# Two places for the front's weight blocks instead of four, the first weights ahead of other transfers, HGRN levels one block later, and only the last row of the last w_down by columns

## The chip, the cores and the metric

One core of a Trainium2 chip runs the whole program. The metric is the device time of one execution in microseconds. Weights come from HBM over 16 DMA engines that the core's queues share; TensorE (PE) multiplies, ScalarE (ACT) and VectorE (DVE) prepare operands and take results, GpSimd (POOL) does small work, and SyncE (SP) issues nearly all transfers, one after the other in the order of the program.

## What the kernel computes

One block of a transformer in float32, 256 tokens of width 1024. The front is a projection of the normed input and two mixers (sparse attention "NSA" and the gated recurrence "HGRN2") whose outputs are merged; then a mixture of 32 experts follows, of which every token uses two:

```
h = rmsnorm(x, attn_norm)
proj = h @ w_in                      # q, kv, gates | hg q, f, i, g | merge
o_nsa = nsa_mixer(...)               # compressed, selected and window attention
o_hg = rmsnorm(hgrn2_mixer(q, f, i, lb), hg_norm) * silu(g)
mixed = sigmoid(m0) * (o_nsa @ w_br_nsa) + sigmoid(m1) * (o_hg @ w_br_hg)
x = x + mixed @ w_out
t = rmsnorm(x, ffn_norm)
x = x + sum_e combine[:, e] * ((silu(t @ w_gate[e]) * (t @ w_up[e])) @ w_down[e])
return rmsnorm(x, final_norm)
```

The experts' weights are 32 x 3 matrices of 2 MB. All of them are read once, whichever tokens choose them.

## The kernel before, in words

**The front.** The weights of the front come in 30 blocks of up to 128x2048 values, in this order: f0, f1, q0, q1 (HGRN forget and query), c0, c1, b0, b1, a0, a1 (NSA), i0, i1, g0, g1 (HGRN value and gate), m20 to m31, h0, h1, m00 to m11, n0, n1 (merge gates and branch outputs), o00, o10, o01, o11 (w_out). Each block takes the same way. SyncE loads it (1.05 MB, tile `raw`, L268, in `load_front`). ScalarE copies it to a value of fewer bits, "hi" (L282), and VectorE takes the rest, "lo" (L286), both into a tile `wsp` (`split`). TensorE then makes a float32 product of three products: hi by hi (L442), hi by lo (L444), lo by hi (L445), in groups of four (`three`), four groups for a block (half as long in c0 and c1). A split runs a block or more ahead of the products, and as its last step it issues the load of a later block into the place that it has read. The raw places are a ring of four halves of two 2 MB buffers.

**Fillers.** Behind each group `run` takes steps from a list (`fill`): the steps of HGRN and NSA. HGRN's are two `hg_diag` (product at L574, then a predicated copy on VectorE) and seven levels of `hg_mm` (product at L600) and `hg_update` (L616, L617, L620 on VectorE); each level's product needs the update of the level before.

**Places for weights.** One pool of eleven 2 MB buffers ("w2", `pair`) holds everything of that size: the raw ring, the `wsp` tiles, the transposed input `hhl`, and the experts' weights. A request takes the buffer that comes free first by the planned order, and a load into it waits for the last reader of what was there. A second pool of three 1 MB buffers ("w", `slot`) holds `x`, the masks `lmf`, `wcm`, the residual's x and w_down's halves `wh`.

**Weights ahead.** `EARLY` says how many pieces of the experts' weights are issued when a block of the front starts. The first quad of experts (24 MB in all) comes as pieces k0 to k3 (a quarter of w_gate's rows for all four experts, L321), u0 to u3 (w_up, L326), and d0, d1, d2 and two halves of the fourth w_down (L331, L339). What isn't loaded early is issued by the experts' products as they free buffers. A SyncE instruction that waits for its buffer holds up all that stand behind it.

**Experts.** Eight quads: gate products `pg` (L1258), up products `pu`, then `py` (L1315), each by four experts side by side. In the last quad w_down is loaded in the parts of `LAST` (L352): rows are the four slices of w_down's rows, columns the output's. `down_last` multiplies rows 0 and 1 for all columns, then rows 2 and 3 in three spans of columns (512, 256 and 256); each span is scaled (`weighted`, L1298 and L1299), added to the output by a product (`scatter`, L1304), squared and normed.

**Start.** SyncE's first transfers are xb (half of the transposed input), f0 in two halves, f1, the vectors and constants, x, q0, the masks and q1. A semaphore lane of a transfer is used again eight transfers later, so eight are under way at most.

## Time and profile before

| | |
|---|---|
| runs shown, lowest, median, highest | 680.13, 681.19, 682.99 us |
| the profiled execution | 680.27 us, span 678.3 us |
| mean granted TensorE clock in it | 0.898 of full speed |
| PE, DVE, ACT busy | 81%, 31%, 21% of the span |
| DMA | 238.84 MB, mean 352 GB/s |
| first expert product to end of span | 243.79 to 678.3 us |

The span is what the engines' records cover; some 2.0 us of the execution lie outside it. The page cuts the span into 40 slices of 17 us: PE is at 8 or 9 tenths through the first 14, the front, while DMA stands at 119 to 254 GB/s in most of slices 3 to 11; from slice 14 on DMA is at 9 tenths or more and PE between 4 and 8. In a timeline each line is one instruction or a run of like ones: its start, its length, engine, line, operation, what it writes and reads, and in brackets how long its engine was idle before it and what released it.

### The profile page before, as it was taken

The page shows a single profiled execution, that of the slowest core. Times are in us where ns is not written, and L with a number is a line of the kernel's source. Part 1 is how long each engine was busy: PE and PEld are TensorE (multiplying, and loading weights), DVE is VectorE, ACT ScalarE, POOL GpSimd, SP SyncE. Part 2 cuts the span into 40 slices and gives each one's busy share as a digit, 9 for nine tenths or more (in the row PEclk, how much of TensorE's full clock was granted, in tenths as well). Part 3 has the DMA queues.
Part 4 walks back from the last instruction along what each step waited for, and adds up shares of the span by engine and source line. Part 5 has one row for each costly group of instructions (what it writes and reads, how often), then busy time and mean ns, then how long its engine had stood idle before and what let it go on. Part 6 is the DMA issues. An engine that isn't in the chain of part 4 may idle for free.

```text
span 678.3 us, 8658 instructions
## 1 busy us (share of the span) xinstructions
PE 548.6 (81%) x3692; PEld 314.8 (46%) x3692; DVE 212.8 (31%) x430; ACT 145.4 (21%) x235; POOL 32.0 (5%) x50
## 2 busy tenths in 40 slices
PE   8989999999999999987758468766846877594574
PEld 6988777888898854342114114212411421141121
DVE  5686856777558342121002102101210110020012
ACT  5433348466455310100000000000000000000003
POOL 0411500200000000000000000000000000000001
PEclk8999999999999999989679788967968796697888
DMA  8856463463578999999999999999999999999993
GB/s 343 346 190 229 143 254 119 151 230 129 191 269 320 425 421 427 427 422 431 427 428 427 426 426 426 429 425 432 423 426 431 422 429 428 426 427 429 420 389 119
DMA packets 26443, 238.84 MB, mean 352 GB/s; under 512 B 2720, under 2 KB 5280, under 8 KB 10144
## 3 DMA queue, kind: packets, MB, share of 16 engines
q1 hardware_dynamic: 26112, 237.44, 84.9%
q8 instruction: 31, 0.51, 0.3%
q10 hardware_dynamic: 288, 0.79, 0.3%
q14 instruction: 12, 0.10, 0.0%
HBM read 237.17 MB, written 1.05 MB: 351 GB/s over the span
## 4 chain that ended last, share of the span: by engine, by line
DMA 50%; PE 29%; DVE 1%; ACT 0%; issue 0%; SPq 0%; POOL 0%; POOLq 0%; DVEq 0%; ACTq 0%
DMA we<-in_w_up 20%; DMA we<-in_w_gate 15%; DMA wh<-in_w_down 10%; DMA wd<-in_w_down 6%; PE pu L1258 5%; PE pws L442 3%; PE pws L445 3%; PE pws L444 3%; PE pg L1258 2%; PE py L1315 2%; PE pga L1146 2%; PE pwo L442 1%; PE pwo L445 1%; PE pwo L444 1%; PE pno L903 1%; PE pnt L880 1%
## 5 line engine op out<-in xcount | busy, mean ns | idle before, releaser
L1258 PE MATMUL pg<-we,xe 128*32 128x512 f32 x512 | 94.3, 723 | 52.1 <-DMA we<-in_w_gate 52.1
L1258 PE MATMUL pu<-we,xe 128*32 128x512 f32 x512 | 91.2, 721 | 47.3 <-DMA we<-in_w_up 43.5
L1286 DVE SCALAR_TENSOR_TENSOR h<-pu,wv,h 128x512 f32<-128x512 f32 x8 | 8.7, 1089 | 246.2 <-PE pu L1258 246.2
L286 DVE TENSOR_TENSOR wsp<-raw,wsp 128x2048 fp32r<-128x2048 f32 (+3 forms) x34 | 68.2, 2011 | 33.7 <-ACT wsp L282 33.5
L1258 PEld LDWEIGHTS pg<-we,xe 128*32 128x32 f32 x512 | 20.1, 128 | 121.7 <-DMA we<-in_w_gate 73.4
L1258 PEld LDWEIGHTS pu<-we,xe 128*32 128x32 f32 x512 | 20.4, 129 | 113.1 <-DMA we<-in_w_up 61.9
L282 ACT ACTIVATE wsp<-raw 128x2048 fp32r<-128x2048 f32 (+3 forms) x34 | 56.3, 1663 | 45.0 <-PE pws L445 14.9
L1298 ACT ACTIVATE ys<-py,wv 128x512 fp32r<-128x512 f32 (+1 forms) x17 | 11.3, 663 | 243.2 <-PE py L1315 211.8
L1315 PE MATMUL py<-wh,hT 128*32 128x512 f32 x112 | 49.4, 594 | 3.7 <-DMA wh<-in_w_down 3.7
L1315 PE MATMUL py<-wd,hT 128*32 128x512 f32 x336 | 50.6, 595 | 0.0
L445 PE MATMUL pws<-hhl,wsp 128*128 128x256 f32 x192 | 49.3, 288 | 0.7 <-DVE wsp L286 0.7
L444 PE MATMUL pws<-hhl,wsp 128*128 128x256 f32 x192 | 49.1, 287 | 0.0
L1280 ACT ACTIVATE h<-pg,wv 128x512 f32<-128x512 f32 x8 | 9.2, 1144 | 150.6 <-PE pg L1258 150.6
L445 PEld LDWEIGHTS pws<-hhl,wsp 128*128 128x128 f32 x192 | 37.4, 195 | 1.0 <-DVE wsp L286 0.9
L444 PEld LDWEIGHTS pws<-hhl,wsp 128*128 128x128 f32 x192 | 37.4, 195 | 0.0
L442 PE MATMUL pws<-hhl,wsp 128*128 128x256 f32 x192 | 34.1, 297 | 1.3 <-ACT hhl L401 1.3
L1299 DVE SCALAR_TENSOR_TENSOR ys<-py,wv,ys 128x512 fp32r<-128x512 f32 (+1 forms) x17 | 12.2, 719 | 69.0 <-ACT ys L1298 68.4
L1146 PE MATMUL pga<-lm,x 128*128 128x128 f32 x256 | 30.3, 276 | 0.0
L444 PE MATMUL pxs<-wsp,hhl 128*128 128x512 f32 (+1 forms) x80 | 29.9, 377 | 0.2 <-DVE wsp L286 0.2
L442 PEld LDWEIGHTS pws<-hhl,wsp 128*128 128x128 f32 x192 | 27.3, 194 | 5.1 <-ACT hhl L401 2.4
L445 PE MATMUL pxs<-wsp,hhl 128*128 128x512 f32 (+1 forms) x80 | 29.5, 372 | 0.0
L1146 PEld LDWEIGHTS pga<-lm,x 128*128 128x128 f32 x256 | 29.3, 192 | 0.2 <-DVE lm L1137 0.2
(252 smaller groups left out, 684.3 us busy)
## 6 DMA issues: line engine op xcount, KB each, us to landing
we<-in_w_gate SPq DMA_DIRECT2D x32, 2048.0 KB, 34.3
we<-in_w_up SPq DMA_DIRECT2D x32, 2048.0 KB, 34.5
wd<-in_w_down SPq DMA_DIRECT2D x21, 2048.0 KB, 39.1
raw<-in_wf SPq DMA_DIRECT2D x27, 1024.0 KB, 4.8
wh<-in_w_down SPq DMA_DIRECT2D x15, 1024.0 KB, 30.0
wd<-in_w_down SPq DMA_DIRECT2D x3, 1024.0 KB, 35.6
wd<-in_w_down SPq DMA_DIRECT2D x3, 512.0 KB, 23.6
wd<-in_w_down SPq DMA_DIRECT2D x6, 256.0 KB, 8.6
```

Of the source, the lines that this page charges most:

```text
L282: i = S.activation(his[n][:, c], raws[n][:, c], AF.Copy)
L286: splits.append((i, V.tensor_tensor(los[n][:, c], raws[n][:, c], his[n][:, c].bitcast(F32), op=OP.subtract)))
L442: PE.matmul(out_, lh, rh, start=start and i == 0, stop=False, skip_group_check=True)
L444: PE.matmul(out_, lh, rl, start=False, stop=False, skip_group_check=True)
L445: last = PE.matmul(out_, ll, rh, start=False, stop=stop and i == n - 1, skip_group_check=True)
L1146: i = PE.matmul(pgs[q, n][:, 128 * k:128 * k + 128], xv[:, tt, 512 * n + 128 * k:512 * n + 128 * k + 128], sel[q][:, tt], start=tt == 0 an ...
L1258: i = PE.matmul(p[32 * e:32 * e + 32], xes[q][:, k, 32 * e:32 * e + 32], W["k", k // 2][:, e, k % 2] if by_rows else W[4 * q + e][:, k], s ...
L1280: S.activation(h, pg.rearrange("p (c j) -> p c j", j=4), AF.Silu, scale=r)
L1286: V.scalar_tensor_tensor(h, pu.rearrange("p (c j) -> p c j", j=4), r, h, op0=OP.mult, op1=OP.mult)
L1298: return (S.activation(hi[:, c], p[:, c], AF.Copy, scale=wv), V.scalar_tensor_tensor(lo[:, c], p[:, c], wv, hi[:, c].bitcast(F32), op0=OP. ...
L1299: V.scalar_tensor_tensor(lo[:, c], p[:, c], wv, hi[:, c].bitcast(F32), op0=OP.mult, op1=OP.subtract))
L1315: PE.matmul(py[n][32 * e:32 * e + 32], hTs[q][:, j, 32 * e:32 * e + 32], WD[4 * q + e, j][:, 512 * n:512 * n + 512], start=j == 0, stop=j ...
```

## The change

The raw ring has two places, halves of one 2 MB buffer, so ten buffers are left for the rest where there were nine. `EARLY` adds two pieces in b0 and n0 and n1 and takes one from i1, 11 in all instead of 9; one more filler per group runs in m20. f0's first half is issued ahead of xb, and vectors, constants, x, masks and wcm are issued behind the latest block. The copy of the token factors (rxb) is put behind VectorE's latest split. In c the first four groups take no filler. `LAST` loads row 2 whole and row 3 in three parts of columns, and `down_last` multiplies rows 0, 1 and 2 for all columns first, and row 3 span by span. The last quad's w_down takes 20 transfers where it took 16: four of 1.05 MB, four of 524 KB, four of 262 KB and eight of 131 KB (before: four of 1.05 MB, four of 524 KB, eight of 262 KB).

```diff
--- before.py
+++ after.py
@@ -171,11 +171,12 @@
 YSB = 4
 WHOLE = slice(0, 512)
 CUTS = [slice(0, 256), slice(256, 512)]
-LAST = [(slice(0, 2), slice(0, 1024)), (slice(2, 4), slice(0, 512)), (slice(2, 4), slice(512, 768)), (slice(2, 4), slice(768, 1024))]
+LAST = [(slice(0, 2), slice(0, 1024)), (slice(2, 3), slice(0, 1024)), (slice(3, 4), slice(0, 512)),
+        (slice(3, 4), slice(512, 768)), (slice(3, 4), slice(768, 1024))]
 GATE_V = (0, 0)
-EARLY = {"a0": 1, "i1": 1, "m31": 1, "m10": 1, "n0": 1, "o00": 1, "o10": 1, "o01": 2}
+EARLY = {"b0": 1, "a0": 1, "m31": 1, "m10": 1, "n0": 2, "n1": 1, "o00": 1, "o10": 1, "o01": 2}
 HOLD = 3
-FILLS = {"n0": 2, "m10": 3, "m20": 1, "m11": 3, "m01": 3, "m00": 3, "h0": 1, "h1": 1, "i": 1, "m30": 1, "g": 1}
+FILLS = {"n0": 2, "m10": 3, "m20": 2, "m11": 3, "m01": 3, "m00": 3, "h0": 1, "h1": 1, "i": 1, "m30": 1, "g": 1}
 
 
 @with_exitstack
@@ -255,24 +256,27 @@
 
     ident = C("ident")
     raws, his, los, marks, splits = {}, {}, {}, [], []
-    ring = [h for _ in range(2) for h in two(pair("raw"), 2048)]
+    ring = two(pair("raw"), 2048)
+    last_dma = []
     to_load, to_split = list(FRONT), list(FRONT)
+
+    def after(i):
+
+        return tc.issue_after(getattr(i, "ins", i))
 
     def load_front():
         if to_load:
             n = to_load.pop(0)
             w = WIDTH[n]
-            raws[n] = ring[FRONT.index(n) % 4][:, :w]
+            raws[n] = ring[FRONT.index(n) % 2][:, :w]
             step = w // 2 if n == FRONT[0] else w
             for o in range(0, w, step):
-                nc.sync.dma_start(raws[n][:, o:o + step], bass.AP(tensor=wf.tensor, offset=wf.offset + FOFF[n] + 128 * o,
-                                                                  ap=[[step, 128], [1, step]]))
+                i = nc.sync.dma_start(raws[n][:, o:o + step], bass.AP(tensor=wf.tensor, offset=wf.offset + FOFF[n] + 128 * o,
+                                                                      ap=[[step, 128], [1, step]]))
+                last_dma.append(i)
                 if n == FRONT[0] and o == 0:
-                    nc.sync.dma_start(xs[1][:, :1024], xb)
-
-    def after(i):
-
-        return tc.issue_after(getattr(i, "ins", i))
+                    with after(i):
+                        nc.sync.dma_start(xs[1][:, :1024], xb)
 
     def split_part(n, c, behind=()):
 
@@ -353,15 +357,16 @@
 
     load_front()
     load_front()
-    nc.sync.dma_start(vc_, vec)
-    nc.sync.dma_start(cs, consts[:, :kept])
-    xv = load_x("x", x)
-    load_front()
-    nc.sync.dma_start(cm_[:, :consts.shape[1] - kept], consts[:, kept:])
-    hgn = row("hgn", cm_[:, 384:])
-    brow = row("br", cp.tile([128, 36], F32, name="brow"))
+    with after(last_dma[-1]):
+        nc.sync.dma_start(vc_, vec)
+        nc.sync.dma_start(cs, consts[:, :kept])
+        xv = load_x("x", x)
     lmf = slot("lmf")[:, :1152].rearrange("p (l t) -> p l t", l=9)
-    nc.sync.dma_start(lmf, lmask)
+    with after(last_dma[-1]):
+        nc.sync.dma_start(cm_[:, :consts.shape[1] - kept], consts[:, kept:])
+        hgn = row("hgn", cm_[:, 384:])
+        brow = row("br", cp.tile([128, 36], F32, name="brow"))
+        nc.sync.dma_start(lmf, lmask)
 
 
     hh_, hl_ = two(pair("hhl", F32R), 2048)
@@ -423,7 +428,8 @@
         prx = bank("ns", "prx")
         with after(marks[-3]):
             PE.matmul(prx[:, :256], one.to_broadcast([128, 128]), rxd, start=True, stop=True)
-        V.tensor_copy(rxb, prx[:, :256])
+        with after(splits[-1][1]):
+            V.tensor_copy(rxb, prx[:, :256])
 
     rt = VC("rt").rearrange("p (k e) -> p k e", k=8)
     G.memset(ones, 1.0)
@@ -432,7 +438,8 @@
         G.tensor_copy(before, lmf[:, 8])
         G.tensor_tensor(rt, rt, VC("fe")[:, :, None].to_broadcast([128, 8, 36]), op=OP.mult)
     wcm = slot("wcm")
-    nc.sync.dma_start(wcm, wcmp)
+    with after(last_dma[-1]):
+        nc.sync.dma_start(wcm, wcmp)
     dump("hT", hhi.bitcast(F32))
 
 
@@ -950,7 +957,10 @@
     hg += [(hg_cross,)]
     for a in hg:
         later(*a)
-    run(project("c", evac_c, 280))
+    gen = project("c", evac_c, 280)
+    for _ in range(4):
+        next(gen)
+    run(gen)
     ns = [(ns_cT, 0), (ns_cT, 1), (ns_blk, 0), (ns_blk, 1)]
     todo[4:4] = [(a[0], a[1:]) for a in ns]
     run(project("b", evac_b))
@@ -1335,9 +1345,9 @@
                               skip_group_check=True)
 
         for i in range(3):
-            products(i, (0, 1))
+            products(i, (0, 1, 2))
         for i, (n, c) in enumerate(spans):
-            products(i, (2, 3))
+            products(i, (3,))
             if i < 2:
                 ys = parts_of()
             weighted(q, n, c, py[i], ys)
```

SyncE, the first transfers of the program, before (`raw` is a block of the front: f0 in two halves, f1, then q0, then q1):

```order
L271 DMA xab<-in_xb 128x1024
L268 DMA raw<-in_wf 128x1024 x2
L268 DMA raw<-in_wf 128x2048
L356 DMA vc__69<-in_vec 128x328
L357 DMA cs<-in_consts 128x202
L229 DMA x<-in_x 128x1024 x2
L268 DMA raw<-in_wf 128x2048
L360 DMA cm__71<-in_consts 128x384
L245 DMA cm__71<-in_rows 128x128
L245 DMA brow<-in_rows 128x36
L364 DMA lmf<-in_lmask 128x1152
L268 DMA raw<-in_wf 128x2048
```

and with the change:

```order
L274 DMA raw<-in_wf 128x1024
L279 DMA xab<-in_xb 128x1024
L274 DMA raw<-in_wf 128x1024
L274 DMA raw<-in_wf 128x2048
L361 DMA vc__69<-in_vec 128x328
L362 DMA cs<-in_consts 128x202
L230 DMA x<-in_x 128x1024 x2
L366 DMA cm__71<-in_consts 128x384
L246 DMA cm__71<-in_rows 128x128
L246 DMA brow<-in_rows 128x36
L369 DMA lmf<-in_lmask 128x1152
L274 DMA raw<-in_wf 128x2048 x2
```

xb goes behind f0's first half, and q0 from ahead of the constants and masks (its place was row 7) to behind them, beside q1.

TensorE at the start of block c, before (`pxs` is c's product, `phl` a step of HGRN):

```order
L442 MATMUL pxs<-wsp,hhl 128x280 x2
L444 MATMUL pxs<-wsp,hhl 128x280
L445 MATMUL pxs<-wsp,hhl 128x280
L444 MATMUL pxs<-wsp,hhl 128x280
L445 MATMUL pxs<-wsp,hhl 128x280
L574 MATMUL phl<-hg_360,hg 128x128 x4
L442 MATMUL pxs<-wsp,hhl 128x280 x2
L444 MATMUL pxs<-wsp,hhl 128x280
L445 MATMUL pxs<-wsp,hhl 128x280
L444 MATMUL pxs<-wsp,hhl 128x280
L445 MATMUL pxs<-wsp,hhl 128x280
L574 MATMUL phl<-hg_360,hg 128x128 x4
```

and with the change, where four groups of c stand ahead of these rows:

```order
L449 MATMUL pxs<-wsp,hhl 128x280 x2
L451 MATMUL pxs<-wsp,hhl 128x280
L452 MATMUL pxs<-wsp,hhl 128x280
L451 MATMUL pxs<-wsp,hhl 128x280
L452 MATMUL pxs<-wsp,hhl 128x280
L581 MATMUL phl<-hg_358,hg 128x128 x4
L449 MATMUL pxs<-wsp,hhl 128x280 x2
L451 MATMUL pxs<-wsp,hhl 128x280
L452 MATMUL pxs<-wsp,hhl 128x280
L451 MATMUL pxs<-wsp,hhl 128x280
L452 MATMUL pxs<-wsp,hhl 128x280
L581 MATMUL phl<-hg_358,hg 128x128 x4
```

The first two steps of HGRN are drawn after the fifth and the sixth group of c instead of after the first and the second.

SyncE, end of the front, before (from the last two blocks but one: `we` are pieces of w_gate and w_up, `wd` and `wh` of w_down):

```order
L268 DMA raw<-in_wf 128x2048 x2
L326 DMA we<-in_w_up 128x4096
L268 DMA raw<-in_wf 128x2048
L326 DMA we<-in_w_up 128x4096
L229 DMA x_1985<-in_xp 128x1024 x2
L326 DMA we<-in_w_up 128x4096 x2
L331 DMA wd<-in_w_down 128x4096
L339 DMA wh<-in_w_down 128x2048
L331 DMA wd<-in_w_down 128x4096 x2
L339 DMA wh<-in_w_down 128x2048
```

and with the change:

```order
L274 DMA raw<-in_wf 128x2048 x2
L330 DMA we<-in_w_up 128x4096
L274 DMA raw<-in_wf 128x2048
L330 DMA we<-in_w_up 128x4096
L274 DMA raw<-in_wf 128x2048
L330 DMA we<-in_w_up 128x4096
L230 DMA x_1987<-in_xp 128x1024 x2
L274 DMA raw<-in_wf 128x2048
L330 DMA we<-in_w_up 128x4096
L335 DMA wd<-in_w_down 128x4096
L343 DMA wh<-in_w_down 128x2048
L335 DMA wd<-in_w_down 128x4096 x2
```

Two of the last three blocks now stand behind the second and third piece of w_up, and o11 behind x.

## Rows read from the trace of the kernel before

**Rows 1.** the page's costliest groups; columns as its line 5 says

```profile
L1258 PE MATMUL pg<-we,xe 128*32 128x512 f32 x512 | 94.3, 723 | 52.1 <-DMA we<-in_w_gate 52.1
L1258 PE MATMUL pu<-we,xe 128*32 128x512 f32 x512 | 91.2, 721 | 47.3 <-DMA we<-in_w_up 43.5
```

**Rows 2.** stretches: from:to, sum, PE, PEld, DVE, ACT, POOL busy, PEclk, DMA share, GB/s

```profile
10.00:20.00 10.00, 10.00 (x73) 9.89 (x72) 8.69 (x17) 7.43 (x12) 0.90 (x2) 0.83 0.91 354
208.00:209.00 1.00, 1.00 (x11) 1.00 (x10) 1.00 (x2) 0.67 (x1) 0.00 (x0) 1.00 0.02 8
210.00:246.00 36.00, 35.54 (x241) 29.43 (x243) 20.54 (x58) 11.02 (x23) 2.01 (x6) 1.00 0.99 412
250.00:260.00 10.00, 10.00 (x80) 3.07 (x72) 2.12 (x7) 2.47 (x2) 0.00 (x0) 1.00 1.01 426
655.00:660.00 5.00, 3.78 (x48) 1.84 (x52) 1.07 (x2) 0.00 (x0) 0.00 (x0) 1.00 1.04 365
660.00:665.00 5.00, 4.85 (x40) 1.49 (x32) 0.75 (x1) 0.69 (x1) 0.00 (x0) 1.00 0.81 264
```

**Rows 3.** timeline of SyncE's queue, end of the front: start, length, instruction

```profile
199.50 0.33 SPq L268 DMA_DIRECT2D raw<-in_wf  x1
209.62 0.33 SPq L326 DMA_DIRECT2D we<-in_w_up  x1
...
245.77 5.48 SPq L326 DMA_DIRECT2D we<-in_w_gate  x4
```

**Rows 4.** timeline of ScalarE, start: start, length, instruction, idle before and releaser

```profile
7.10 0.63 ACT L282 ACTIVATE wsp<-raw 128x512 fp32r<-128x512 f32 x1 [4.44 <-DMA raw<-in_wf]
...
16.76 1.92 ACT L282 ACTIVATE wsp<-raw 128x2048 fp32r<-128x2048 f32 x1 [1.34 <-DMA raw<-in_wf]
...
25.55 1.91 ACT L282 ACTIVATE wsp<-raw 128x2048 fp32r<-128x2048 f32 x1 [6.78 <-DMA raw<-in_wf]
```

**Rows 5.** timeline of SyncE's queue, start

```profile
6.21 0.43 SPq L268 DMA_DIRECT2D raw<-in_wf  x1
...
11.72 1.56 SPq L268 DMA_DIRECT2D raw<-in_wf  x2
```

**Rows 6.** timeline of TensorE, first products of q0 and of q1

```profile
22.50 0.82 PE L442 MATMUL pws<-hhl,wsp 128*128 128x256 f32 x4
...
28.43 0.64 PE L442 MATMUL pws<-hhl,wsp 128*128 128x256 f32 x4
```

**Rows 7.** waits of TensorE, 0 to 60 us: total, times, longest

```profile
PE phl L574 <- DVE hg L564: 1.4, 1, 1.4
PE pws L442 <- ACT hhl L401: 1.3, 1, 1.3
PE pws L445 <- DVE wsp L286: 0.7, 1, 0.7
PE phl L600 <- DVE cdav L575: 0.6, 1, 0.6
PE phl L600 <- DVE hg L617: 0.5, 1, 0.5
```

**Rows 8.** VectorE's half of a split, L286: durations min/median/max in ns, shapes

```profile
L286 DVE TENSOR_TENSOR wsp<-raw,wsp x34: 680/2289/2648, 7.8 to 219.8; 128x2048 fp32r<-128x2048 f32 x26, 128x512 fp32r<-128x512 f32 x4, 128x1024 fp32r<-128x1024 f32 x2, 128x1120 fp32r<-128x1120 f32 x2
```

**Rows 9.** the page's transfers: KB each, median us from issue to landing

```profile
raw<-in_wf SPq DMA_DIRECT2D x27, 1024.0 KB, 4.8
```

**Rows 10.** timeline of TensorE, first products of o01 and of o11

```profile
220.34 0.62 PE L442 MATMUL pwo<-wsp,mT 128*128 128x512 f32 x2
...
225.78 0.62 PE L442 MATMUL pwo<-wsp,mT 128*128 128x512 f32 x2
```

**Rows 11.** timeline of ScalarE, tail: scalings of the last products

```profile
663.24 0.69 ACT L1298 ACTIVATE ys<-py,wv 128x512 fp32r<-128x512 f32 x1 [28.59 <-PE py L1333]
...
668.57 0.47 ACT L1298 ACTIVATE ys<-py,wv 128x256 fp32r<-128x256 f32 x1 [0.74 <-PE py L1333]
```

**Rows 12.** waits of ScalarE, 0 to 30 us

```profile
ACT wsp L282 <- DMA raw<-in_wf: 12.6, 3, 6.8
```

## The prediction

> **What bounds the kernel now.** I read the page's slices and its costliest groups first, then stretches of the span, then the queues at both ends of the front, then the tail. The groups show the second half waiting for weights: both expert products spend about half as long idle as busy, and a weight transfer ends that idle time [rows 1]. The stretches show the rate there, 426 GB/s, so from some point on the end is fixed by bytes [rows 2]. That point is what matters. The transfer engines last stand still in 208 to 209 us (8 GB/s); from 210 they are never idle again, and 210 to 246 moves 36 us x 412 GB/s = 14.83 MB [rows 2]. In SyncE's queue o11's block goes out at 199.50, and the next weights, waiting for a place, only at 209.62 [rows 3]. From there to 245.77 it issues six 2.10 MB pieces, two 1.05 MB ones and 1.05 MB of x: 15.73 MB. So at 245.77 about 1 MB is still under way, 2.3 us at 426 GB/s, and the stream would run dry at 248.1. At 245.77 the first expert product frees the first place and the queue goes on without a gap [rows 3]. All eleven places are full by then.
>
> Hence two limits, and the later one rules: the stream as loaded until then (dry at 248.1), and the moment of the first release, which hangs on TensorE's chain through the front. Before, the first was later by 2.3 us. A change in the front is worth what it does to the later of the two, and a weight fetched early is worth nothing by itself, for the places are full in both versions at the first release and the bytes left are the same.
>
> **The change, part by part.**
>
> *The first transfers.* f0's first half no longer shares the start with xb. ScalarE waited 4.44 us for it, to 7.10 [rows 4]; xb is 0.52 MB, 1.2 us at 426 GB/s, so I take 1.2 us off. It closes nearly all of TensorE's 1.3 us wait for the first operand [rows 7]. TensorE's granted clock was 0.83 in 10 to 20 us [rows 2], between the two levels 1.2 and 2.4 GHz; if that goes, up to 1.7 us more is won, and if it grows as much is lost. I count 0.
>
> *q0 goes behind the masks.* With two places q0's load waits for f0's split. It was issued at 6.21 [rows 5] and reached ScalarE at 16.76 [rows 4], 10.5 us later. Now it is issued at some 12.4, behind 0.87 MB that it used to precede. Lower end: bytes alone, 0.87 MB at 354 GB/s [rows 2] or 2.5 us more than before, so ready at 19.2. Upper end: it takes as long as q1 did, issued at 11.72 [rows 5] and ready at 25.55 [rows 4], 13.8 us, so 26.2. With q0's own 10.5 us it is 22.9. I take 21, between the bytes and its own time. Then the two halves of the split take 1.9 us [rows 4] and 2.3 us [rows 8]: hi at 22.9, lo at 25.2. TensorE, at q0 from 22.50 - 1.2 = 21.3, waits for both, and after the first 0.5 us of products has 5.4 of its 5.9 us [rows 6] left at 25.2: end 30.6 instead of 28.43, +2.2. Then q1's split is no longer late, and its 0.7 us wait [rows 7] goes: +1.5. With the ends 19.2 and 26.2 it is -0.3 and +6.7.
>
> *HGRN levels a block later.* In c TensorE waited 1.4, 0.6 and 0.5 us for VectorE's operands of the first levels [rows 7]. Four groups of c now stand ahead of the first level, some 3 us of products, which covers the longest wait; one short wait remains at the next level's update, which I price with the 0.6 us row. Gain 1.9 us. The steps queued behind the levels are later by as much, beside blocks b and a, whose products cover them. At the end of c the chain is then 1.5 - 1.9 = -0.4.
>
> *Two places for all later blocks.* A block's load now waits for the split two blocks before. The split runs a block ahead of the products, 1.9 + 2.3 = 4.2 us; so when the split of the block two before ends, the new block's products are three blocks less 4.2 us away: 3 x 5.9 - 4.2 = 13.5 us [rows 6], and its own split must start 4.2 us sooner. That leaves 9.3 us for a landing of 4.8 us [rows 9], or of 9.7 behind a 2.10 MB piece (4.9 us at 426 GB/s), or of 14.6 behind two. In the queue at most one piece stands directly ahead of a block, and pieces wait for places themselves: I take 0, with 0 and 5.3 (two pieces, once) as ends. The Trainium skill's page "DMA: Bandwidth & Descriptors", in its rules for kernel authors, says to issue a transfer early and wait for it late, so that its fixed cost lies beside work; halving the places goes against that. By it the loads would surface in the front as in the second rival below; the trace of before, with four places, cannot show it.
>
> *o11's split.* Its product buffer now shares an address with o01's, and the split can start only when o01's last product ends at 225.78 [rows 10]; hi at 227.7, lo at 230.0. TensorE has work for some 3.2 of these 4.2 us (transposes, the hi products now drawn together, router products): +1.0, with 0.3 and 2.5 as ends. ScalarE and VectorE stand behind it with nothing that anyone needs sooner.
>
> So the first release moves by -0.4 + 1.0 = +0.6, to 246.4; new transfers then need some 0.8 us to flow (210 to 246 lost (426 - 412) / 426 x 36 = 1.2 us to its start at most [rows 2]): 247.2.
>
> *The stream.* SyncE gets a place freed by o00's split rather than by n1's end, so it starts 1.5 us earlier, and the front is 0.4 earlier there; one 2.10 MB piece less and two blocks more are the same bytes. It is dry at 248.1 - 1.9 = 246.2. The later limit is the release: 247.2 against 248.1, -0.9.
>
> *The last w_down.* The first scaling of a product is at 663.24 and the last at 668.57 [rows 11]. Row 2 whole and row 3 cut finer leaves half the products behind each last piece: 0.4 us less on TensorE at the end, but the first scaling waits for row 3 and comes about 2 us later, on ScalarE, whose chain of squares ends the kernel. I take -0.4. The rate fell from 426 to 365 and 264 GB/s while the pieces shrank to 512 and 256 KB [rows 2]; now the last eight are 128 KB. Ends: -1.3 if they fly as before and the piece is short, +1.1 if the last 1.05 MB goes at 264 instead of 365 GB/s. The same page of the Trainium skill asks for at least 1 MiB per transfer; the falling rates agree, and by its measured 341 GB/s at 1 MB and 138 at 64 KB the last 1.05 MB would take an estimated 3.1 to 7.6 us.
>
> Sum: -0.9 - 0.4 = -1.3 us. Profiled execution 680.27 (span 678.3 and 2.0 outside it), so 679.0. The median of the runs shown is 0.9 higher; I forecast 679.5 in between.
>
> **Rivals.** (1) *The extra place pays in full*: a 2.10 MB piece more is in before experts begin, 4.9 us at 426 GB/s, 675.4. For it: the engines stood still at 208 to 209. Against: 1 MB was still under way at the first release, so a release 2.3 us sooner gains what the stream gains, and it needs the chain: with q0's low end the release is at 244.6, transfers at 245.4, -2.7, and with the tail's good end too -4.0, 676.3. (2) *The front starves*: a block lands after its turn, at q0 (19.1 to 26.2) or behind the weight pieces ahead of n0 and the o blocks. Place: the first release. From a release at 247.3 on (0.8 before 248.1) each microsecond goes through to the end. With q0's upper end the release moves by 6.7 - 1.9 + 1.0 = +5.8, to 251.6, transfers at 252.4: +4.3, less the tail's 0.4, 684.2 on the profiled execution and 685.1 on the median. For it: q1's 13.8 us and ScalarE's 6.8 us wait for it. Against: only three transfers of blocks were waited for in the whole front, all before 26 us [rows 4, 12]. (3) *Nothing but the tail shows*: chain and stream cancel, 680.
>
> **Chances.** Mine and (3), which share an outcome, 0.62; (1), whole or half, 0.22; (2), with the tail's bad end, 0.16. A measurement of this kernel tells about 0.5%, 3.4 us, from no change: faster than 677.8 takes (1), slower than 684.6 takes (2). The likeliest case alone is 677.6 to 681.5; for 8 in 10 the range reaches 676.3 to 683.8.
>
> **What would show it.** Right: ScalarE's wait for the first block near 3 us, q0 at ScalarE near 21, no wait of TensorE above 0.7 us in c, o11's first product at some 227.7, the release near 246.4, and the same 426 GB/s from there. Wrong: waits of ScalarE for a block past 30 us; a release beyond 248; or a stream that stands still before the release for longer than a microsecond, which would say that the places, not the chain, rule.

## The result and the profile after

Over 15 runs of each, the changed kernel takes 683.77 us (682.51 to 686.13) and the kernel before 680.13 us (678.52 to 682.99): a ratio of 1.0058, with a 95% interval from 1.0049 to 1.0068, 3.9 us slower by the ratio. The forecast was 679.5, range 676.3 to 683.8: a small gain was forecast and a loss came, and that the median still lies 0.03 us inside the range is luck. The profiled execution took 686.13 us, span 684.0. It is the slowest of the 15, and in it products of the last weights ran at the lower of TensorE's two clocks (rows at the end); that this is what made it the slowest is not shown. For the tail a second profile of the same kernel (681.40 us, the run e11 below) stands beside it. Times of e3 below leave out one execution of 1194.26 us. "Release" below is the start of SyncE's transfer of four w_gate pieces, the first behind the first expert product.

Step by step, with the forecast's own terms:

| place | before | forecast | after | |
|---|---|---|---|---|
| first product of TensorE | 8.19 | about 1.2 earlier | 6.52 | held |
| q0 at ScalarE | 16.76 | 21 | 21.34 | held |
| q0's last product ends (q1's first starts) | 28.43 | 30.6 (+2.2) | 33.48 (+5.05) | **failed** |
| c starts, without its HGRN gain | 35.10 | +1.5 | 39.24 (+4.14) | follows |
| c's start to o00's start | 174.33 | -1.9 | 171.04 (-3.3) | more; differs between executions |
| o00's start to the release | 36.34 | +1.0 | 39.97 (+3.63) | **failed** |
| release | 245.77 | 246.4 | 250.25 (+4.48) | |
| stream dry | 248.1 | 246.2 | about 250.1 | **failed** |
| release to the end | 434.5 | 432.6 | 435.9, second profile 432.3 | held in the second |

**The start.** ScalarE's timeline of the changed kernel (columns as in [rows 4]), with f0, q0 and q1:

```profile
5.44 0.63 ACT L286 ACTIVATE wsp<-raw 128x512 fp32r<-128x512 f32 x1 [2.78 <-DMA raw<-in_wf]
...
21.34 1.91 ACT L286 ACTIVATE wsp<-raw 128x2048 fp32r<-128x2048 f32 x1 [6.85 <-DMA raw<-in_wf]
23.82 1.91 ACT L286 ACTIVATE wsp<-raw 128x2048 fp32r<-128x2048 f32 x1 [0.58 <-DMA raw<-in_wf]
```

The wait for f0 is 2.78 us instead of 4.44, and that for q1, 6.78 us before [rows 4], has moved to q0, with 6.85 us. What q0's wait does is on TensorE, whose timeline has the first products behind it:

```profile
23.30 0.74 PE L449 MATMUL pws<-hhl,wsp 128*128 128x256 f32 x4 [3.04 <-ACT wsp L286]
...
25.62 0.58 PE L452 MATMUL pws<-hhl,wsp 128*128 128x256 f32 x1 [1.47 <-DVE wsp L290]
```

It waits 3.04 us for hi and, after one group, 1.47 us for lo. The stretches of the changed kernel around it (columns as in [rows 2]):

```profile
24.00:26.00 2.00, 0.53 (x3) 0.38 (x2) 1.97 (x3) 1.74 (x1) 0.00 (x0) 0.69 0.26 111
26.00:28.00 2.00, 2.00 (x11) 2.00 (x11) 2.00 (x2) 0.63 (x1) 0.00 (x0) 0.50 0.70 224
28.00:30.00 2.00, 2.00 (x11) 2.00 (x11) 2.00 (x5) 0.00 (x0) 0.00 (x0) 0.50 0.28 90
30.00:32.00 2.00, 2.00 (x13) 2.00 (x12) 0.41 (x2) 1.66 (x2) 0.61 (x1) 0.60 0.72 260
32.00:34.00 2.00, 2.00 (x19) 2.00 (x19) 0.31 (x1) 0.00 (x0) 0.00 (x0) 1.00 0.00 0
```

The number of products, in the first brackets of each row, is the reading: TensorE is busy throughout, but from 26 to 32 it does 11, 11 and 13 products in 2 us, and 19 once the granted clock is 1.00 again. That is 35 products instead of 57, and 22 x 2 / 19 = 2.3 us lost at 1.2 instead of 2.4 GHz.

**The o blocks.** ScalarE before, from the split of o00 to that of o11 (L282 is the hi half of a split, L999 the copy of the merged columns `mT`, the o blocks' other operand):

```profile
201.93 1.90 ACT L282 ACTIVATE wsp<-raw 128x2048 fp32r<-128x2048 f32 x1
...
205.25 1.18 ACT L999 ACTIVATE mT<-mg 128x512 fp32r<-128x512 f32 x2
206.75 1.92 ACT L282 ACTIVATE wsp<-raw 128x2048 fp32r<-128x2048 f32 x1 [0.32 <-PE pws L445]
211.00 1.23 ACT L999 ACTIVATE mT<-mg 128x512 fp32r<-128x512 f32 x2 [2.33 <-DVE mg L997]
213.85 1.92 ACT L282 ACTIVATE wsp<-raw 128x2048 fp32r<-128x2048 f32 x1 [1.62 <-DVE wsp L286]
217.81 1.92 ACT L282 ACTIVATE wsp<-raw 128x2048 fp32r<-128x2048 f32 x1 [2.05 <-PE pwo L445]
```

and after (L286 and L1009 are the same two):

```profile
206.11 1.17 ACT L1009 ACTIVATE mT<-mg 128x512 fp32r<-128x512 f32 x2 [1.68 <-DVE mg L1007]
207.19 1.90 ACT L286 ACTIVATE wsp<-raw 128x2048 fp32r<-128x2048 f32 x1
209.43 0.63 ACT L1009 ACTIVATE mT<-mg 128x512 fp32r<-128x512 f32 x1 [0.34 <-DVE mg L1007]
213.56 0.63 ACT L1009 ACTIVATE mT<-mg 128x512 fp32r<-128x512 f32 x1 [3.50 <-DVE mg L1007]
214.10 1.90 ACT L286 ACTIVATE wsp<-raw 128x2048 fp32r<-128x2048 f32 x1
216.57 1.91 ACT L286 ACTIVATE wsp<-raw 128x2048 fp32r<-128x2048 f32 x1 [0.58 <-PE pwo L452]
...
228.78 1.91 ACT L286 ACTIVATE wsp<-raw 128x2048 fp32r<-128x2048 f32 x1 [0.88 <-ACT sqs L1053]
```

Before, the split of o00 stands ahead of the first copies and that of o10 ahead of the second. After, each stands behind: o00's by 5.3 us, o10's by 7.4, and the latter now waits out the 3.50 us that a copy waits for VectorE. The weights were not what they waited for: o00's had been issued at 194.59, o10's at 200.40, and no split here waits for a transfer. The splits in turn free the raw places, so SyncE issues o01 at 211.62 and o11 at 218.35, where the last block went out at 199.50 before [rows 3]:

```profile
211.62 0.33 SPq L274 DMA_DIRECT2D raw<-in_wf  x1
...
218.35 0.33 SPq L274 DMA_DIRECT2D raw<-in_wf  x1
...
250.25 5.48 SPq L330 DMA_DIRECT2D we<-in_w_gate  x4
```

TensorE's timeline of the changed kernel has the waits that come of it:

```profile
211.65 0.50 PE L451 MATMUL pwo<-wsp,mT 128*128 128x512 f32 x1 [0.27 <-DVE wsp L290]
...
218.38 0.50 PE L451 MATMUL pwo<-wsp,mT 128*128 128x512 f32 x1 [0.98 <-DVE wsp L290]
...
229.48 0.66 PE L1067 MATMUL pxt<-cs,x 128*128 128x128 f32 x4 [0.34 <-DVE x L1045]
230.75 1.18 PE L449 MATMUL pwo<-wsp,mT 128*128 128x512 f32 x4 [0.61 <-ACT wsp L286]
```

Before, it waited 0.46 us in this stretch (`h2T`, there after too). Now 2.2 us of listed waits come on top. By pieces the 3.63 us are: o00 takes 6.04 us (5.47 before), o10 6.77 (5.44), o01 5.44 (5.44), and o11 with the router up to the first expert product 19.73 (18.01). What makes up the 1.4 us beyond the listed waits is not shown. The split of o11 starts at 228.78, when o01's last product (228.30, 0.40 long) has ended; the row names ScalarE's own instruction before it, but e7 below, with the same wait of 0.88 us, names the product.

**The stream.** Stretches of the changed kernel from o01's load to behind the release:

```profile
212.00:214.00 2.00, 2.00 (x10) 1.66 (x9) 1.49 (x3) 0.44 (x1) 0.00 (x0) 1.00 0.58 180
214.00:250.00 36.00, 33.60 (x221) 26.91 (x224) 18.07 (x50) 11.47 (x23) 3.49 (x6) 1.00 1.01 426
250.00:252.00 2.00, 2.00 (x24) 0.65 (x20) 1.21 (x10) 0.01 (x1) 0.00 (x0) 1.00 0.64 168
252.00:254.00 2.00, 2.00 (x24) 0.65 (x20) 0.00 (x0) 0.00 (x0) 0.00 (x0) 1.00 0.79 311
254.00:264.00 10.00, 10.00 (x87) 3.18 (x76) 1.83 (x7) 2.48 (x2) 0.00 (x0) 1.00 1.01 426
```

Half microseconds around the release show when it ran dry:

```profile
249.50:250.00 0.50, 0.50 (x8) 0.13 (x4) 0.50 (x7) 0.50 (x5) 0.00 (x0) 1.00 0.96 377
250.00:250.50 0.50, 0.50 (x12) 0.20 (x8) 0.50 (x7) 0.01 (x1) 0.00 (x0) 1.00 0.28 115
250.50:251.00 0.50, 0.50 (x12) 0.19 (x8) 0.47 (x5) 0.00 (x0) 0.00 (x0) 1.00 0.12 49
251.00:251.50 0.50, 0.50 (x12) 0.13 (x4) 0.24 (x1) 0.00 (x0) 0.00 (x0) 1.00 1.60 360
```

That is at about 250.1, just as the release comes (250.25), and new transfers flow some 0.8 us after it, as forecast. They come up slowly, though: at 426 GB/s the 168 and 311 of 250 to 254 are 0.8 and 1.5 us of transfers, so 1.7 us are lost there. The stream ran dry 3.9 us later than forecast, and it started 3.5 us too late: o01's raw load, which waits for o00's split, and the weights behind it go out from 211.62, where 208.1 was forecast (209.62 less 1.5) and 209.62 was before. The raw load at 218.35 waits for a split too, but over 214 to 250 the rate is 426 GB/s. From 254 on it is that of before [rows 2].

### The profile page after: what moved, and what is told of

It reads as the page before. It is cut to its first block, busy times and chain, and to the rows that moved or that the text cites. A ratio compares the mean times of both kernels' runs of the same rounds, so it can differ in the third digit from the quotient of the medians.

```text
span 684.0 us, 8668 instructions
## 1 busy us (share of the span) xinstructions
PE 551.1 (81%) x3692; PEld 315.8 (46%) x3692; DVE 212.2 (31%) x430; ACT 142.6 (21%) x233; POOL 30.2 (4%) x50
## 2 busy tenths in 40 slices
DMA packets 25483, 238.84 MB, mean 349 GB/s; under 512 B 2784, under 2 KB 4320, under 8 KB 9184
## 3 DMA queue, kind: packets, MB, share of 16 engines
HBM read 237.17 MB, written 1.05 MB: 348 GB/s over the span
## 4 chain that ended last, share of the span: by engine, by line
DMA 49%; PE 43%; DVE 4%; ACT 2%; issue 1%; POOL 0%; SPq 0%; POOLq 0%; ACTq 0%; DVEq 0%
DMA we<-in_w_up 21%; DMA we<-in_w_gate 10%; DMA wd<-in_w_down 10%; DMA wh<-in_w_down 5%; PE pu L1268 5%; PE py L1325 4%; PE pws L449 4%; PE pws L452 4%; PE pws L451 3%; DMA raw<-in_wf 3%; PE pxs L449 2%; PE pga L1156 2%; PE pxs L451 2%; PE pxs L452 2%; DVE wsp L290 1%
## 5 line engine op out<-in xcount | busy, mean ns | idle before, releaser
L1268 PE MATMUL pg<-we,xe 128*32 128x512 f32 x512 | 92.8, 710 | 51.9 <-DMA we<-in_w_gate 51.9
L1268 PE MATMUL pu<-we,xe 128*32 128x512 f32 x512 | 94.0, 738 | 48.3 <-DMA we<-in_w_up 44.7
L286 ACT ACTIVATE wsp<-raw 128x2048 fp32r<-128x2048 f32 (+3 forms) x34 | 56.2, 1662 | 53.2 <-PE pws L452 23.5
L452 PE MATMUL pws<-hhl,wsp 128*128 128x256 f32 x192 | 49.9, 290 | 1.5 <-DVE wsp L290 1.5
L451 PE MATMUL pws<-hhl,wsp 128*128 128x256 f32 x192 | 49.9, 290 | 0.0
L452 PEld LDWEIGHTS pws<-hhl,wsp 128*128 128x128 f32 x192 | 38.1, 199 | 1.7 <-DVE wsp L290 1.7
L451 PEld LDWEIGHTS pws<-hhl,wsp 128*128 128x128 f32 x192 | 38.1, 199 | 0.2 <-issue 0.2
L449 PE MATMUL pws<-hhl,wsp 128*128 128x256 f32 x192 | 34.6, 299 | 4.0 <-ACT wsp L286 3.0
L449 PEld LDWEIGHTS pws<-hhl,wsp 128*128 128x128 f32 x192 | 27.6, 196 | 8.5 <-ACT wsp L286 3.4
(252 smaller groups left out, 679.5 us busy)
```

The costliest lines, as they stand in the source:

```text
L286: i = S.activation(his[n][:, c], raws[n][:, c], AF.Copy)
L449: PE.matmul(out_, lh, rh, start=start and i == 0, stop=False, skip_group_check=True)
L451: PE.matmul(out_, lh, rl, start=False, stop=False, skip_group_check=True)
L452: last = PE.matmul(out_, ll, rh, start=False, stop=stop and i == n - 1, skip_group_check=True)
L1268: i = PE.matmul(p[32 * e:32 * e + 32], xes[q][:, k, 32 * e:32 * e + 32], W["k", k // 2][:, e, k % 2] if by_rows else W[4 * q + e][:, k], s ...
```

## The experiments

Each ratio is against the kernel before on the same chip; release and segments are of each run's profile.

**The parts.** The two edits that don't touch the places, each alone on the kernel before; then everything but the places and what hangs on them; then only the places with the new start.

```diff
# e5_hgrn: before, and only
-    run(project("c", evac_c, 280))
+    gen = project("c", evac_c, 280)
+    for _ in range(4):
+        next(gen)
+    run(gen)
# e6_last: before, and only LAST and down_last as in the change
# e1_noring: the change, but
-    ring = two(pair("raw"), 2048)
+    ring = [h for _ in range(2) for h in two(pair("raw"), 2048)]
#   (and EARLY, FILLS, rxb and the order of the constants, q0 and masks of before)
# e2_ring: the change, without HGRN's later start and without the new LAST
```

> The kernel before with the HGRN shift alone. From c's first product to o00's first the three-part kernel needed 170.8 us where the kernel before needs 174.3, and the changed kernel 171.0 where the one without the shift needed 175.6: theory A says the shift is worth 3.5 us in any of them, 676 to 677 us, first release near 242.5. Rival B (the 1.9 us that the three waits in c add up to): 678 to 678.5 us. Rival C (the shift helps only beside an earlier start): 679.5 to 680.5 us.

Measured: 677.81 us (677.60 to 680.48), ratio 0.9968 [0.9957, 0.9979]. The release comes at 244.41, 1.36 us earlier; the ratio says 2.2 us, with 1.4 to 2.9 by its interval. The term of -1.9 lies within that. Theory A's 3.5 us lies outside that interval. Of TensorE's waits for the first levels one of 1.0 us is left, where the forecast left 0.6.

> The kernel before with the new cut of the last w_down alone. Theory A: no gain or loss that can be told, 679.4 to 680.4 us: the profiled three-part kernel ended as much earlier (2.55 us) as its first release came earlier, so its tail took the same time. Rival B (a tail with 131 KB pieces is slower): 681 us or more. Rival C (it is worth the forecast 0.4 or its good end of 1.3): 678.6 to 679.5 us.

Measured: 679.32 us (677.49 to 681.00), ratio 0.9993 [0.9983, 1.0003]: nothing that can be told, with the forecast's -0.4 inside. SyncE's queue of the two goes with that; the rows are the last transfer of w_down and the last of the output, first before, then with LAST alone:

```profile
661.21 0.37 SPq L352 DMA_DIRECT2D wh<-in_w_down  x1
672.87 0.35 SPq L1397 DMA_DIRECT2D out_dram<-fin  x1
673.60 0.35 SPq L1394 DMA_DIRECT2D out_dram<-fin  x1
```

```profile
663.18 0.33 SPq L353 DMA_DIRECT2D wh<-in_w_down  x1
672.84 0.34 SPq L1398 DMA_DIRECT2D out_dram<-fin  x1
673.57 0.34 SPq L1395 DMA_DIRECT2D out_dram<-fin  x1
```

From the last piece to the output it is 2.0 us shorter, and the last of the smaller pieces goes out 2.0 us later.

> The kernel before with the three other parts alone: f0's first half ahead of xb, HGRN levels four groups later, the last w_down cut as in the change; four places in the ring, early pieces and masks as before. Theory A (the two places cost the time: q0 late at the start, and in the o blocks splits that stand behind the mT copies): these parts are harmless, 677.5 to 680 us, first release (SyncE's g4) at 243 to 246 us. Rival B (the tail with its 131 KB transfers, or the HGRN order, costs it): 682 us or more with the first release near 245.8.

Measured: 676.77 us (675.80 to 677.74), ratio 0.9952 [0.9937, 0.9966], release 243.22, o00's start to release 36.33 us as before (36.34). It is a little faster than theory A's range.

> The changed kernel without the HGRN shift and without the new cut of the last w_down: what is left is the two places, the early pieces and the order of the first transfers. Theory A: the whole loss is here, 683.5 to 686 us, first release at 250 us or later (the HGRN waits of c come on top of the late q0). Rival B: 680 to 681.5 us.

Measured: 688.71 us (686.66 to 689.34), ratio 1.0120 [1.0101, 1.0139], release 255.62, o00's start to release 39.91 us. So the loss lies in the bundle of places, early pieces, start, FILLS and rxb, and the other edits hide part of it. It is 2.7 us above theory A's range. The change, which has HGRN's later start and the new LAST besides, is 4.2 us below it by the ratios, where the two alone gave 2.2 and 0.5 us on the kernel before; from c's start to o00's start it is 175.64 us without them and 171.04 with them.

**The two stalls.** e3 gives q0 and q1 places of their own and loads q0 ahead of the masks; e4 only puts the copies of the merged columns behind the splits of o00 and o10; e7 does both.

```diff
# e3_q4 (and e7)
+    first4 = two(pair("raw2"), 2048)
-            raws[n] = ring[FRONT.index(n) % 2][:, :w]
+            raws[n] = (first4 if FRONT.index(n) in (2, 3) else ring)[FRONT.index(n) % 2][:, :w]
...
         xv = load_x("x", x)
+    load_front()
# e4_defer (and e7)
-                S.activation(hi, g, AF.Copy)
-                V.tensor_tensor(lo, g, hi.bitcast(F32), op=OP.subtract)
+                pend.append((i, j, g))    # emitted behind splits[-1] when n1 and o00 start
```

> The changed kernel, but q0 and q1 are loaded into two places of their own, which go back to the pool after q1's split; q0 is issued ahead of the masks as in the kernel before. Theory A: the start's share goes (o00 begins 2.5 to 4 us earlier than 210.3: the wait of 3 us for q0's hi, 1.5 for its lo and the lower clock behind them, and the 1.2 us won at f0 stays), the o blocks' 1.9 us and o11's 1.65 stay: 681 to 682.5 us, first release near 247. Rival C (q0's late landing is the whole loss): 679 to 680 us. Rival D (the stream that runs dry rules, not the chain): 683 to 684 us, unchanged.

Measured: 680.46 us (677.40 to 684.36), ratio 1.0011 [0.9991, 1.0031]. q0 is at ScalarE at 16.55 and c starts at 33.10 instead of 39.24; o00 starts at 206.22, 4.1 us earlier than in the change. From o00 to the release it is still 39.94 us. By the ratios the start is worth 3.2 us of the 3.9 that the change lost, in the parts that theory A names, though its range for the time was missed by half a microsecond. q0 is not the whole loss, since the o blocks keep theirs.

> The changed kernel, but the copies of the merged branch into mT (ScalarE and VectorE) are put behind the splits of o00 and o10, the order that the kernel before had; the work is the same. Theory A: o00 and o10 take 5.45 us each again instead of 6.0 and 6.8, first release 1.5 to 2.5 us earlier than 250.25, stream too because o01's load waits for o00's split: 681.5 to 682.5 us. Rival C (q0 is the whole loss): 683.5 to 684 us, no change.

Measured: 681.73 us (680.43 to 684.41), ratio 1.0031 [1.0020, 1.0042]; o00 to release 38.38 us, 1.6 less than the change. That is the price of the order on ScalarE; 2.04 us against the 36.34 of four places remain. The release itself, at 251.38, is later than the change's 250.25 and not earlier as expected: this profile is the slowest of the twelve, and its front reaches o00 only at 213.00 (210.28), with a granted clock of 0.83 in 50 to 60 us where the change has 1.00.

> The changed kernel with both repairs: places of their own for q0 and q1, and the mT copies behind the splits of o00 and o10. Theory A: they add up, o00 begins near 206 us, from there to the first release 38.4 us instead of 39.9 (what is left against 36.3 is o11's split, which still waits for o01's last product): 679 to 679.8 us, and still behind the three-part kernel's 676.8, since the places themselves win nothing. Rival B (the eleven early pieces do pay once the front doesn't suffer): 676.5 us or less.

Measured: 677.11 us (675.87 to 678.81), ratio 0.9957 [0.9942, 0.9972]; o00 to release 38.40 us. It is 2 us faster than expected. The segments add up: o00 starts at 206.29 as in e3, and from there it is what e4 took. By the ratios the two repairs are worth 3.2 and 1.8 us alone and 6.9 together; an excess of 1.9 us is no more than these intervals leave open. The result is that of e1: two places with both repairs win nothing on four.

**What remains in the o blocks.** In e7 o11's split still waits for o01's last product. Leaving out one early piece changes which address it gets, so that it waits only for o10's. Two such kernels, and the change once more:

```diff
# e9_ten_b0: e7, but "b0": 0 in EARLY
# e10_ten_n1: e7, but "n1": 0 in EARLY
# e11_after_again: the change, unaltered
```

> The change with both repairs (q0 and q1 in places of their own ahead of the masks, the merged columns' copies behind the splits of o00 and o10), and with ten expert pieces ahead of the router instead of eleven: block b0 starts none. In the program's waits, o11's split then no longer waits for o01's last product but for o10's. Theory (the 2.05 us that the two places still cost between o00's start and the first release are o11's split, which shares its address with o01's): from o00's start to the first release 36.3 to 36.6 us instead of 38.40, TensorE waits nothing for o11's split (0.6 us with eleven), release about 242.6, time 675.0 to 676.5 by the release, or up to 677.1 where the stream running dry sets the end. Rival (the transfer of o01's or o11's raw weights, issued late for want of a place, is what costs it): 38.2 to 38.5 us there as with eleven, time 677 to 678.

> As the run with b0's piece left out, but the piece left out is n1's, which stands some 100 us later. Theory (o11's split shares its address with o01's): from o00's start to the first release 36.3 to 36.6 us, whichever piece is left out, time within 0.5 us of the other's. Rival (the place of the raw weights): 38.2 to 38.5 us, since the raw weights of o01 and o11 are issued as late as before; if one of the two shortens and the other doesn't, it is the order of the transfers and not the address.

> The changed kernel again, beside the two above on one chip, for a profile nearer to its median: span some 681.5 to 682.5 us, from o00's start to the first release 39.9 to 40.0, q0 at ScalarE at 21.3 to 22.5, c's start at 39 to 40, from the release to the end 433 us. If the last products again run at half the clock, the tail of the first profile was no chance of one execution.

Measured: e9 683.47 us (681.90 to 684.01), ratio 1.0047 [1.0032, 1.0062]; e10 679.73 us (676.81 to 682.34), 1.0000 [0.9983, 1.0016]; e11 684.24 us (681.08 to 686.55), 1.0066 [1.0043, 1.0089]. From o00 to the release e9 takes 39.46 us, e10 36.55 and e11 39.92. Here is o11's split on ScalarE in e7, in e10 and in e9:

```profile
223.24 1.91 ACT L287 ACTIVATE wsp<-raw 128x2048 fp32r<-128x2048 f32 x1 [0.88 <-PE pwo L455]
```

```profile
218.49 1.92 ACT L287 ACTIVATE wsp<-raw 128x2048 fp32r<-128x2048 f32 x1 [4.20 <-DMA raw<-in_wf]
```

```profile
224.29 1.91 ACT L287 ACTIVATE wsp<-raw 128x2048 fp32r<-128x2048 f32 x1 [8.40 <-DMA raw<-in_wf]
```

In e7 a product of o01 releases it; in e10 the transfer does, 4.75 us sooner, and the segment is back within 0.2 us of four places. So the shared address was the 1.9 us in e7. In e9, where the address is free too, the transfer of o11 is there only 10.7 us after its issue (213.60, behind a w_up piece at 209.24 and x), 16.4 us after o00's start; in e7 the address had held the split to 17.0 us after it. TensorE waits 1.50 us for hi and 0.69 us for lo. The expectation's own rule would read one shortened and one unshortened segment as the transfers' order and against the address; the releasers say that each is a limit, one right behind the other. All expected times missed: e10 gained 1.9 us at the release and nothing at the end, e9 was worse from block b on, and e11's start was shorter than expected (c at 38.02). In e9 o00 starts at 207.90 instead of 206.29, and the piece that b0 no longer starts leaves the transfer engines little to do there: 107 GB/s in 40 to 50 us where e7 has 308. e10 still has two places, and its 36.55 us say that two places as such cost the o blocks 0.2 us; the 3.6 came with the instruction order and the addresses that went with them.

**Four places with the repaired start.** The last kernel keeps the ring of four and EARLY of before, issues f0 ahead of xb and q0 and q1 ahead of the masks, and has HGRN's later start and the new LAST (and rxb's place of the change).

```diff
# e8_q1first: the change, but with ring, EARLY and FILLS of before, and
         xv = load_x("x", x)
+    load_front()
+    load_front()
```

> Four places again, the three other parts, the vectors and masks behind f0 and f1 as in the change, and now q0 and q1 both ahead of the masks. In the three-part kernel q1's split was late: q1 took 9.0 us instead of 5.8, part of it at the lower clock level. Theory A (what the first blocks' landing sets, TensorE's chain passes on to the first release and to the end): c begins near 32 us instead of 36.1, first release 239 to 241, 672.5 to 674.5 us. Rival B (the masks become late and HGRN's first levels wait for them): 676 to 677 us, as the three-part kernel, with waits of TensorE for a step of HGRN in c above 1.5 us. Rival C (the stream of weights rules by then and runs dry first): first release earlier, but end 675 to 676.5 us.

Measured: 675.45 us (674.67 to 677.00), ratio 0.9932 [0.9919, 0.9945]: the fastest of all, ahead of both kernels. Its ScalarE gets q0 and q1 at

```profile
16.56 1.91 ACT L286 ACTIVATE wsp<-raw 128x2048 fp32r<-128x2048 f32 x1 [2.67 <-DMA raw<-in_wf]
...
20.43 1.91 ACT L286 ACTIVATE wsp<-raw 128x2048 fp32r<-128x2048 f32 x1 [1.86 <-DMA raw<-in_wf]
```

and c starts at 32.03 (35.10 before), the release comes at 241.31, and o00 to release is 36.33 us. The theory's time was missed by a microsecond and its release by 0.3; the rival by which the stream and not the release sets the end holds.

**One measure for all of them.** The stretch from 0 to 264 us, behind the point where the stream flows in most of them, in before, e2, the change (e11) and e8; the last number is the mean rate:

```profile
0.00:264.00 264.00, 256.14 (x1867) 212.69 (x1868) 165.08 (x328) 121.60 (x197) 29.81 (x42) 0.99 0.66 257
```

```profile
0.00:264.00 264.00, 251.04 (x1824) 211.54 (x1828) 165.44 (x327) 121.22 (x197) 31.63 (x42) 0.99 0.63 243
```

```profile
0.00:264.00 264.00, 253.16 (x1863) 211.08 (x1864) 164.67 (x328) 118.86 (x195) 28.02 (x42) 0.99 0.65 254
```

```profile
0.00:264.00 264.00, 260.32 (x1896) 215.86 (x1897) 168.30 (x332) 119.32 (x195) 27.46 (x42) 0.99 0.68 264
```

Each GB/s is 0.264 MB, and 238.84 MB in all must pass; what is left goes at 427 GB/s (300 to 600 us of before and after alike). So for before 264 + (238.84 - 67.85) / 0.427 = 664.4, and the execution ended 15.9 us later.

| | GB/s to 264 | bytes done at | profiled end | difference |
|---|---|---|---|---|
| before | 257 | 664.4 | 680.27 | 15.9 |
| change (e11) | 254 | 666.3 | 681.40 | 15.1 |
| e2 | 243 | 673.1 | 688.71 | 15.6 |
| e4 | 250 | 668.8 | 684.41 | 15.6 |
| e9 | 251 | 668.2 | 683.82 | 15.6 |
| e1 | 261 | 662.0 | 677.72 | 15.7 |
| e7 | 261 | 662.0 | 678.04 | 16.0 |
| e10 | 261 | 662.0 | 678.84 | 16.8 |
| e8 | 264 | 660.1 | 677.00 | 16.9 |

In these nine the difference keeps within 2 us while the ends spread over 12. Over the other profiles it is 14.8 (e3) to 17.3 (e5), and 18.6 in the change's first, with its slow tail: over all thirteen it spreads by 3.8 us, as much as the change lost, so the number orders large differences and not small ones, and no run tested it by changing the bytes alone. e10 and e7 show what this says: a release 1.9 us earlier with one piece fewer on its way is the same number of bytes, and the profiled ends are 0.8 us apart.

## Why the prediction was wrong, point by point

- **q0's wait was priced as a wait alone.** "End 30.6 instead of 28.43, +2.2" took its landing right (21 forecast, 21.34 measured) and let the remaining 5.4 us of products run at full clock, which would have ended at 31.0 from the measured 25.62. They ended at 33.48: the granted clock was 0.50 after the 3.04 and 1.47 us of waiting. With this the chain's "+1.5" at c became +4.14. The clock was spoken of for 10 to 20 us and "I count 0"; a wait that the text itself had placed at q0 had to carry it. e3 and e8 show that it hangs on q0: with q0 at 16.55 and 16.56 c starts at 33.10 and 32.03, and the granted clock of both is 1.00 from 20 to 40 us. The loss at the lower clock is not the same each time: e11, with waits of 2.99 and 1.47 us, reaches c 1.22 us sooner.

The Trainium skill, in "TensorE: Matmul & The Clock Gate", section "HAM oscillation — how this bites in real kernels", describes a kernel in which the wait for a transfer between two groups of products makes the next group start at half clock. The rows of 26 to 32 us agree: 0.50, 0.50 and 0.60 behind the waits for q0's split.

- **"Two places for all later blocks: I take 0" failed, and "o11's split +1.0" was too small.** From o00 to the release the change, e2 and e3 take 3.6 us more than the kernels with four places (36.33 to 36.35). Of it 1.6 is ScalarE's order (e4 against the change), 1.9 is o11's split behind o01's last product (e10 against e7), inside the forecast's ends of 0.3 and 2.5, and 0.2 is left with two places (e10). The step reckoned with landings, and a late landing was not what came first: the order written for ScalarE had put two splits behind copies that wait for VectorE, though the weights were there. The moves stood in the order of ScalarE's instructions, and the prediction read that of SyncE and TensorE only. Why the order came out so was not tried; that a plan with fewer places expects the blocks later is only argued.
- **The stream, "dry at 246.2", was dry at about 250.1.** The term counted SyncE's start 1.5 us earlier, and not that a raw load that waits for a split (211.62) stands in the same queue ahead of the weights: the stream started 2.0 us later than before instead.
- **The frame held.** The later of two limits decides: the release moved 4.48 us and the stream with it, and in the profiles of kernels with eleven early pieces where the tail wasn't slow it is 432.3 to 433.4 us from the release to the end, against 432.6 forecast. Rival (2), the front that starves, is the nearest to what happened: its places (q0, the o blocks) were right, and its 685.1 on the median is 1.3 us from 683.77, but that is partly chance: q0 landed as forecast and not at its upper end, and the loss came by the clock behind it and the splits' order. What stood against it, that only three transfers were waited for, said nothing on either.
- **Held:** f0's first half (first product 1.67 us earlier, 1.2 forecast), HGRN's levels (2.2 us alone by the ratio, 1.9 forecast; c's start to o00's start takes 170.8 to 174.4 us in the profiles that have them later and 174.3 to 175.6 in the others), the last w_down (nothing measurable, -0.4 forecast).
- **The signs.** Of those named for right, ScalarE's wait for the first block (2.78), q0 at ScalarE and the 426 GB/s came; "no wait of TensorE above 0.7 us in c" and o11's first product at 227.7 did not (1.13 us at 47.69, for VectorE; 230.75). Of those for wrong, the release beyond 248 came, and one wait of ScalarE for a block past 30 us (5.04, to 42.75); TensorE waited for no block there.
- **Rival (1), the extra place pays, is borne out by no kernel here:** with both repairs (e7) the time equals that of four places without it (e1), with o11's split freed as well (e10) it is no better, and e8 with four is 1.7 us below e7, with a start that is 1.3 us shorter too.

Open: e10's median is 2.6 us above e7's though their bytes and profiles nearly agree. The filler added in m20, rxb's place and the early pieces of n0 and n1 were not run alone on the kernel before.

## What to carry to other kernels

Read a changed order for every engine that frees a buffer, not only for those that wait: here the splits on ScalarE freed the places and had moved 5 and 7 us, while TensorE waited only 0.27 and 0.98 us for their data. Waits of 3.04 and 1.47 us between products cost the waits here and then 2.3 us of products at half clock, and 1.2 us less in another execution, so write both into the sum, the second with a range. And where a long stretch is bound by transfers, count the bytes landed at one time behind its start: in the pair e7 and e10 a release 1.9 us earlier without more bytes gained nothing.

## What the runs showed of the hardware

- After waits of 3.04 and 1.47 us, with 0.53 us of products in 24 to 26, six microseconds of products ran at 1.2 GHz (granted 0.50, 0.50 and 0.60 in two-microsecond stretches). In the second profile of the same kernel the stretch 20 to 30 was granted 0.83 instead of 0.74 and c started at 38.02 instead of 39.24: what such a wait costs differs by a microsecond between executions.
- The tail differs between executions too. In the changed kernel's first profile the last quad's products ran at the lower clock in this stretch, and in its second not:

```profile
650.00:655.00 5.00, 4.34 (x24) 1.06 (x28) 0.00 (x0) 0.00 (x0) 0.00 (x0) 0.50 1.01 414
```

```profile
650.00:655.00 5.00, 5.00 (x46) 1.30 (x38) 0.00 (x0) 0.00 (x0) 0.00 (x0) 1.00 1.01 415
```

24 and 46 products at the same transfer rate; the release to the end took 435.9 and 432.3 us. This goes together and is not shown to be cause and effect: e5, e9 and e10 take 436.1 to 436.5 us there as well. Among the 15 runs the six with a mean clock of 0.900 or more took 682.51 to 683.88 us, the four with 0.892 or less 684.62 to 686.13.
- Transfers of 131 KB cost the last w_down nothing that the times show (0.9993): its last piece went out 2.0 us later, and the end came as before.
